# Attention scores: the low part of the keys padded with zero rows, so that both passes of a score use all 128 rows

## The chip, the cores and the metric

The kernel runs on one core of a Trainium2 chip. The metric is the device time of one execution in microseconds (us). Three runs of the kernel before took 2261.57, 2261.72 and 2266.63 us, so their median is 2261.72 us.

## The reference

The reference runs two blocks on 256 tokens x of 1024 features, the first of them together with 256 context tokens. All values are float32. The first block holds, in this order, a feed-forward layer, a differential attention, two more feed-forward layers, a neighbourhood attention and another feed-forward layer. The second block has two hybrid layers, which the change does not touch. The two attentions matter here:

```python
def _diff_attend(q, k, v, lam):                  # 8 heads, each with two halves j of 64 features
    s = jnp.einsum('bthjd,bkhjd->bhjtk', q, k)   # the scores
    p = jax.nn.softmax(s, axis=-1)
    p = p[:, :, 0] - lam * p[:, :, 1]
    return jnp.einsum('bhtk,bkhe->bthe', p, v)

# neighbourhood attention: 16 heads of 64 features, queries of x alone
s_lat = jnp.einsum('bqhd,brkhd->bhqrk', q, kb) + bias
s_ctx = jnp.einsum('bqhd,bchd->bhqc', q, kc)
p = jax.nn.softmax(concatenate([s_ctx, s_lat]))
```

In the differential attention the queries of x see 512 keys and those of the context see the 256 keys of the context. In the neighbourhood attention each query of x sees 512 keys.

## The kernel before

TensorE multiplies operands of the type float32r. A float32 value is held as the sum of two float32r parts, high and low, and a product takes three passes: high by high, high by low, low by high (`mm3`, L190; each matmul is issued in `mm`, L161, so most matmuls of the trace stand at L164).

A score has only 64 features to sum over, half of the 128 rows of the array. `stack` (L692) uses this to need two passes instead of three. For each half j of a pair of 64 features, the rows that the half owns are `own` (rows 0 to 63 for j = 0, rows 64 to 127 for j = 1). The tile `a` (named w in the trace) holds the high part of the query on the rows `own` and its low part on the other 64 rows. The tile `b` (also w) holds the high part of the key on both. The tile `kl` holds the low part of the key, on the rows `own` alone, for j = 0 and j = 1 in the two halves of the partitions of one [128, 512] tile. ScalarE makes the high parts (L699, L700, and the copy on the other rows, L703), VectorE makes the low parts by subtraction (L701, L702).

`score` (L706) then issues two matmuls into one PSUM bank. The first runs over all 128 rows and gives high by high plus low by high. The second takes the 64 rows `own` of `a` and of `kl` and gives high by low. In the trace they are `ac<-w` and `ac<-kl,w`.

In the differential attention (`diff_attention`, L730) each of 8 heads has four tiles of 128 queries and two halves, so 8 scores: four over 512 keys and four over 256. A head's work: `project` takes the finished projections of queries and keys out of PSUM (L743, L744), applies the rotary embedding on VectorE (L747 to L750) and calls `stack`; `values` transposes the previous head's probabilities (L200, L786) and multiplies them with the values (L179); `scores` issues the 8 scores with the maximum on VectorE (L765), the exponential on ScalarE (L766) and the normalisation on VectorE (L767 to L770). The generator `projections` issues the next head's projections (`ab<-u,w`, 48 matmuls a head), which the scheduler lays between the scores. Each engine runs its instructions in the order that is fixed when the program is built.

In the neighbourhood attention (`nb_attention`, L814) each of 8 head pairs has two tiles of queries and two heads, so 4 scores over 512 keys. The rest is alike: L825 and L826 take out the projections, L839 to L850 are the softmax, L864 takes out the transposes.

The memory of such a stage comes from a pool that is opened after the feed-forward layer before it; the first writes into it wait for the last readers of the tiles that lay there.

Of the kernel before, what the change touches and what calls it, by code (L numbers as in the profile page):

```python
# [23 lines left out]
F = mybir.dt.float32  # L24
R = mybir.dt.float32r
# [7 lines left out]
FA = 12  # L33
# [10 lines left out]
class Split:  # L44
    """A float32 operand held exactly as the sum of two float32r parts."""
# [8 lines left out]
class Sums:  # L54
    """sums of squares over the 1024 features of 256 tokens, from four parts [128, 2, 256]: the parts added
    up on the vector engine or, direct, on the tensor engine"""
# [27 lines left out]
class Net:  # L84
# [16 lines left out]
    @contextmanager  # L101
    def psum(self, **tags):
        """The PSUM banks of a phase: a number for each kind of use."""
        with ExitStack() as es:
            self.banks = self.pool(es, "ps" + "_".join(tags), 1, space=bass.MemoryType.PSUM)
            self.nbank = tags
            yield

    @contextmanager
    def space(self, name, n):  # L110
        """The 4 KiB tiles of a phase."""
        with ExitStack() as es:
            self.bp = self.pool(es, name, n)
            yield

    # ---- tiles
# [21 lines left out]
    # ---- weights: raw float32 from DRAM, then two float32r parts that sum to it  # L138
# [19 lines left out]
    # ---- products. A start clears the flags of its whole bank. Groups that share a bank are run one  # L158
    # after another (groups=0), or as one group (groups=n) whose first matmul alone has the start and
    # whose last alone the stop.  # L160
# [28 lines left out]
    # out += stat^T @ mov for every (out, mov), in three passes of float32r  # L189
# [12 lines left out]
    # ---- constants  # L202
# [27 lines left out]
    # ---- modulation vectors: ada_w^T silu(c) + ada_b, as columns  # L230
    def ada_first(self):
        """The first layer's first scale and the last quarter of its shift on the tensor engine, the rest of
        the shift on the vector engine. Returns x's norm factors."""
# [45 lines left out]
    def ada_chunks(self, l, mods):  # L279
        """Thunks, one for each 128 values of modulation, and one for each vector that adds the bias."""  # L280
# [31 lines left out]
    def spread(self, thunks, steps):  # L312
        """An iterator: each next() runs its share of the thunks."""
        thunks = list(thunks)
        done = 0
        for i in range(steps):
            want = -(-(i + 1) * len(thunks) // steps)
            while done < min(want, len(thunks)):
                thunks[done]()
                done += 1  # L320
            yield
        while True:
            yield

    # ---- norm factors as columns
    def pre_cols(self, l, which, j):
        """(1 + scale) * g and shift of sublayer `which` (0, 1, 2) for half j."""
        a = self.const([128, DT], f"pa{l}{which}{j}", tag=f"pa{which}{j}")
        self.nc.vector.scalar_tensor_tensor(a, self.mod[l][:, 3 * which + 1, :, j], 1.0, self.ng[l][:, 2 * which],
                                            op0=OP.add, op1=OP.mult)  # L330
        return a, self.mod[l][:, 3 * which, :, j]
# [7 lines left out]
    # ---- 1 / sqrt(sum of squares / n + eps) in every partition: a table's value and one Newton step  # L339
    def rstd(self, ss, n, p=None):  # L340
        """ss: tensors whose sum is to be summed over the partitions, if p, that sum in PSUM, isn't given"""
# [25 lines left out]
    def add_normed(self, y, r, cols, j):  # L367
        """h += cols * rmsnorm(y), y in two tiles [128, 4, 256]"""
# [12 lines left out]
    def table(self, x):  # L381
        """loads the table of the inverse root, once x is there"""
        self.nc.scalar.activation(self.col.tile([128, 1], F, name="tb", tag="tb", bufs=1), x, AF.Abs_reciprocal_sqrt)

    def new_u(self, n=2):
        """hi and lo of [1024, 256 n] features by tokens"""
# [16 lines left out]
    def normed(self, u, cols, shift, j, r=None, dve=False):  # L403
        """u = rmsnorm(h) * cols + shift in two parts"""
# [18 lines left out]
    def scaled(self, cols, shift=None):  # L423
        """h * cols of x in two parts, with shift's parts in the two columns that follow, if there is one, and
        the factors 1 / rms(h) of the tokens, along the free dimension in every partition"""
# [17 lines left out]
    def columns(self, r):  # L443
        """r as columns [128 tokens, 2]"""
# [7 lines left out]
    # ---- feed-forward  # L452
    def ffn(self, n, u, halves, mid, xdone, extra=(), r=None):
        """xdone(y) takes x's tiles of silu(a) * b @ w_out, then ctx's are worked out and returned.
        mid() is run when the work on x that needs nothing of ctx has been issued."""
# [51 lines left out]
        with self.space("ffn", 12):  # L507
# [19 lines left out]
            # the first FA features' share of y  # L527
# [11 lines left out]
            # the others', x before ctx  # L539
# [27 lines left out]
    # ---- shared parts of the mixers  # L567
# [10 lines left out]
    def projections(self, src, u, first):  # L578
        """starts the products of a mixer's queries (x's alone, if first is 1) and keys. The generator
        prefetches the weights of the next pair before it gives a pair's PSUM; the first pair's x comes  # L580
        apart, before ctx."""
# [20 lines left out]
    def v_tiles(self, src, u, mid, more):  # L602
        """token-major values [128 tokens, 1024] of the four token tiles, x's before mid()"""
# [31 lines left out]
    def out_proj(self, src, o, halves, xdone):  # L635
        """o(h, j) gives the pair [128, 256] of rows 128 h .. of the product's input for half j. The steps
        of the first quarter are given out, for use while o is still being made."""
# [52 lines left out]
    # ---- products of two 64-row operands, two to a tile: q = qh + ql stands on the rows of both halves,  # L690
    # so that one pass carries qh kh + ql kh and a second one qh kl
    def stack(self, q, k, tile_):  # L692
# [3 lines left out]
        kl = tile_((128, nk), "kl")  # L696
        for j in range(2):
# [4 lines left out]
            nc.vector.tensor_tensor(kl[own], k[own], b[own, j].bitcast(F), op=OP.subtract)  # L702
            nc.scalar.activation(b[other, j], k[own], AF.Copy)  # L703
        return a, b, kl

    def score(self, s, ops, j, q0, q1, k0, k1):  # L706
        a, b, kl = ops
        own = slice(64 * j, 64 * j + 64)
        self.mm(s, a[:, j, q0:q1], b[:, j, k0:k1], True, False)
        self.mm(s, a[own, j, q0:q1], kl[own, k0:k1], False, True)  # L710

    # ---- differential attention
# [17 lines left out]
    def diff_attention(self, u, mid, xdone):  # L730
        nc, I = self.nc, self.I
        with self.space("da", 1):
            rope = self.big((128, 2, 256), tag="rope")
            nc.sync.dma_start(rope, I["rope"].rearrange("a p t -> p a t"))
            rc, rs = [rope[:, i].unsqueeze(1).broadcast_to([128, 2, 256]) for i in range(2)]
            qks = self.projections(I["da_qk"], u, 2)
# [3 lines left out]
            def project():  # L740
# [10 lines left out]
                return self.stack(qk[:, 0], qk[:, 1],  # L751
                                  lambda shape, tag: self.bp.tile(list(shape), R, name=tag, tag=tag, bufs=1))
# [60 lines left out]
    # ---- neighbourhood attention (queries of x alone)  # L813
    def nb_attention(self, u, mid, xdone):  # L814
        nc, I = self.nc, self.I
        with self.space("na", 1):
            tile_ = lambda shape, tag, bufs, dt=F: self.bp.tile(list(shape), dt, name=tag, tag=tag, bufs=bufs)
            qks = self.projections(I["na_qk"], u, 1)
# [3 lines left out]
            def project():  # L822
# [4 lines left out]
                return self.stack(qk[:, 0:256], qk[:, 256:768], lambda shape, tag: tile_(shape, tag, 1, R))  # L827
# [64 lines left out]
    # ---- the second block's layer  # L892
    def softmax_small(self, rows, scale, bias, n, e):
        """softmax over n keys of scale * (the scores in PSUM + bias), into e"""
# [8 lines left out]
    def causal_pair(self, q, k, v, scale, bias, gate, x):  # L903
        """x [128, 256] = gate * the two heads' causal attention, a head in each 64 partitions:
        q(j), k(j) feature-major, v(j, tt) token-major [128, 64], bias(j, qt) over 128 (qt + 1) keys"""
# [24 lines left out]
    def second_consts(self):  # L930
# [12 lines left out]
        # sel[:, k] spreads row k of every block of 16 rows over the block  # L943
# [31 lines left out]
    def gates(self, ba, abt):  # L975
        """beta and the log decay of GDN, token-major [128 tokens, 2 tiles, 4 heads]"""
# [11 lines left out]
        # log1p(e) = ln(w) + (e - (w - 1)) / w with w = 1 + e  # L988
# [12 lines left out]
    def delta_rule(self, prn, cw, gates, abt, others):  # L1001
        """Returns U and the causal q k matrix: o^T = U^T A, by the two tiles of tokens."""
# [22 lines left out]
        # decays between tokens j <= t, then the two triangular matrices, transposed: [j, t]  # L1025
# [36 lines left out]
        # inverses of the diagonal blocks, dd = (1 + N)^-1 and ee its transpose: blocks of 16 column by column,  # L1062
        # row k of a block spread over the block's rows by the tensor engine, then larger ones from pairs
# [45 lines left out]
        # values token-major, then both blocks' solutions  # L1109
# [20 lines left out]
    def rope_pe(self, x, n):  # L1130
        """in place on partitions 64 .. 95 of x [128, n, 256]"""
# [9 lines left out]
    def hybrid(self, l, scaled, prm3):  # L1141
# [35 lines left out]
        # MLA  # L1177
# [46 lines left out]
        # MoBA: the one block is the queries' own, so it is causal attention with the T5 bias  # L1224
# [13 lines left out]
        # GDN output  # L1238
# [24 lines left out]
        # h += the heads' product, the last heads after all others  # L1263
# [16 lines left out]
    # ---- the whole  # L1280
# [40 lines left out]
    def first_block(self, es, on, ada):  # L1321
# [10 lines left out]
        with self.psum(ab=3, ac=4):  # L1332
            # silu(c) along the free dimension, in every partition
# [13 lines left out]
            # u of the next sublayer from the last one's y (or none), for one half  # L1347
# [67 lines left out]
# ---- layout on the host  # L1415
# [43 lines left out]
def layout(v):  # L1459
    """The kernel's input arrays from the reference's: moved values and constants of the shapes alone."""  # L1460
# [29 lines left out]
    # the bias of every (query, key) of x: a value of the table inside the window, else the reference's constant  # L1490
# [9 lines left out]
    # second block  # L1500
# [47 lines left out]
```

## Time and profile before

| | |
|---|---|
| median of 3 runs (lowest, highest) | 2261.72 us (2261.57, 2266.63) |
| span of the profiled execution | 2263.0 us |
| instructions | 33412 |
| TensorE matmuls (PE), busy | 2206.7 us, 98% |
| TensorE weight loads (PEld), busy | 1884.7 us, 83% |
| VectorE (DVE), busy | 1590.9 us, 70% |
| ScalarE (ACT), busy | 1121.4 us, 50% |
| GpSimd (POOL), busy | 4.4 us |
| differential attention, first to last score | 476.8 to 643.6 us of the span |
| neighbourhood attention, first to last score | 1498.8 to 1622.9 us of the span |

The page gives no time for the profiled execution beside its span of 2263.0 us; that lies 1.3 us above the median of the runs and inside their range. Each matmul has its own weight load, and loads overlap matmuls. Matmuls are pipelined, so the lengths of neighbouring ones overlap in the timeline; the distance from one matmul's start to the next one's tells more than the length of one.

### The profile page before, as it was taken

Reading aid. Unit: us, or ns where it says so; the run is one execution under the profiler, and the core shown is the slowest. Engines: PE = TensorE matmul, PEld = TensorE weight load, DVE = VectorE, ACT = ScalarE, POOL = GpSimd, SP = SyncE. Lnnn points to the kernel's source line nnn. Section 1 sums busy time; section 2 is a strip of 40 time slices with the busy share of each in tenths; the row PEclk is TensorE's granted clock in tenths of the full one; section 3 lists DMA queues with packets and bytes.
Section 4 is the critical chain, followed back from the end, with each engine's and each line's share of the span. In section 5 each row is a group of like instructions: output and inputs, shape, how many; then the busy total and the mean of one; then the engine's idle time right before and its main releaser. Section 6 shows DMA issues by size and latency. Waiting matters only on the chain.

```text
span 2263.0 us, 33412 instructions
## 1 busy us (share of the span) xinstructions
PE 2206.7 (98%) x13010; PEld 1884.7 (83%) x13010; DVE 1590.9 (70%) x2899; ACT 1121.4 (50%) x1841; POOL 4.4 (0%) x29
## 2 busy tenths in 40 slices
PE   7999999999999999999999999999999989999998
PEld 4888889876679988889988889977789989888986
DVE  7876665868869876767854454956666568977985
ACT  4332224667768322235632233667654448547744
POOL 0000000000000000000000000000000000000000
PEclk9999999999989999999999999999999999999999
DMA  8555553421124755544554553432235553324321
GB/s 304 196 185 188 180 183 131 145 93 47 38 93 134 235 197 190 195 166 150 177 187 151 175 167 131 149 130 85 94 134 184 177 170 121 113 75 137 121 98 56
DMA packets 96164, 332.75 MB, mean 147 GB/s; under 512 B 12772, under 2 KB 15462, under 8 KB 96008
## 3 DMA queue, kind: packets, MB, share of 16 engines
q1 hardware_dynamic: 96008, 330.64, 43.0%
q8 instruction: 102, 1.67, 0.3%
q14 instruction: 54, 0.44, 0.1%
HBM read 329.55 MB, written 1.05 MB: 146 GB/s over the span
## 4 chain that ended last, share of the span: by engine, by line
PE 85%; DVE 7%; ACT 5%; DMA 1%; issue 1%; SPq 0%; DVEq 0%; ACTq 0%
PE ab L164 39%; PE ac L164 17%; PE ac L168 7%; PE pj L164 5%; PE ab L179 5%; PE gd L164 3%; PE n L164 3%; PE ab L168 2%; DVE w L156 1%; PE at L164 1%; ACT w L155 1%; PE gd L168 1%; DVE y L375 1%; PE pj L168 1%; DVE h L379 1%
## 5 line engine op out<-in xcount | busy, mean ns | idle before, releaser
L155 ACT ACTIVATE w<-raw 128x1024 fp32r<-128x1024 f32 x466 | 489.4, 1053 | 792.7 <-PE ab L164 271.9
L164 PE MATMUL ab<-u,w 128*128 128x512 f32 (+2 forms) x4320 | 876.2, 362 | 4.1 <-ACT u L438 4.1
L164 PEld LDWEIGHTS ab<-u,w 128*128 128x128 f32 x4320 | 727.2, 189 | 133.2 <-issue 5.1
L156 DVE TENSOR_TENSOR w<-raw,w 128x1024 fp32r<-128x1024 f32 x466 | 567.1, 1219 | 321.8 <-ACT w L155 314.9
L164 PE MATMUL ac<-b,w 128*128 128x512 f32 (+1 forms) x1152 | 235.9, 366 | 0.0
L164 PEld LDWEIGHTS ac<-b,w 128*128 128x128 f32 x1152 | 195.6, 188 | 39.6
L168 PE MATMUL ac<-b,w 128*128 128x256 f32 x1680 | 200.6, 280 | 0.0
L168 PEld LDWEIGHTS ac<-b,w 128*128 128x128 f32 x1680 | 198.4, 188 | 0.8
L164 PE MATMUL pj<-u,w 128*128 128x256 f32 (+1 forms) x1200 | 159.4, 289 | 5.6 <-ACT u L438 4.4
L293 DVE SCALAR_TENSOR_TENSOR ra<-ra,cb 128x1024 f32<-128x1024 f32 x130 | 158.2, 1221 | 5.5 <-ACT cb L1342 2.2
L164 PEld LDWEIGHTS pj<-u,w 128*128 128x128 f32 (+1 forms) x1200 | 148.7, 191 | 10.7 <-ACT u L438 5.0
L179 PE MATMUL ab<-u,w 128*128 128x256 f32 x1152 | 147.6, 290 | 7.6 <-ACT u L155 6.2
L179 PEld LDWEIGHTS ab<-u,w 128*128 128x128 f32 x1152 | 144.2, 197 | 9.2 <-ACT u L155 6.5
L293 DVE SCALAR_TENSOR_TENSOR c<-ra,cb 128x1024 f32<-128x1024 f32 x98 | 118.7, 1218 | 11.9 <-ACT cb L1342 6.4
L484 DVE TENSOR_TENSOR s<-s,ab 128x512 f32<-128x512 f32 (+1 forms) x78 | 47.0, 603 | 90.7 <-PE ab L164 90.2
L164 PE MATMUL ac<-w,u 128*128 128x512 f32 x384 | 90.4, 393 | 0.0
L164 PE MATMUL n<-r,ones 128*128 128x256 f32 (+1 forms) x216 | 77.4, 470 | 7.5 <-DVE r L62 3.1
L164 PEld LDWEIGHTS ac<-w,u 128*128 128x128 f32 x384 | 71.7, 188 | 15.4 <-DVE u L156 0.4
L155 ACT ACTIVATE b<-s 128x512 fp32r<-128x512 f32 (+1 forms) x100 | 53.5, 535 | 26.9 <-DVE s L484 19.8
L156 DVE TENSOR_TENSOR b<-s,b 128x512 fp32r<-128x512 f32 (+1 forms) x100 | 56.2, 562 | 3.1 <-ACT b L155 2.9
L164 PEld LDWEIGHTS n<-r,ones 128*128 128x128 f32 x216 | 37.7, 203 | 21.4 <-DVE r L62 9.4
L64 ACT ACTIVATE r<-h 128x512 f32<-128x512 f32 x56 | 35.1, 628 | 31.7 <-DVE h L379 10.7
(289 smaller groups left out, 2311.2 us busy)
## 6 DMA issues: line engine op xcount, KB each, us to landing
raw<-in_fin SPq DMA_DIRECT2D x194, 512.0 KB, 3.3
raw<-in_fout SPq DMA_DIRECT2D x112, 512.0 KB, 3.3
ra<-in_ada SPq DMA_DIRECT2D x72, 512.0 KB, 4.3
ra<-in_ada0r SPq DMA_DIRECT2D x58, 512.0 KB, 3.3
raw<-in_w SPq DMA_DIRECT2D x54, 512.0 KB, 3.3
raw<-in_da_qk SPq DMA_DIRECT2D x16, 512.0 KB, 3.2
raw<-in_na_qk SPq DMA_DIRECT2D x16, 512.0 KB, 3.3
raw<-in_w2o SPq DMA_DIRECT2D x16, 512.0 KB, 3.2
```

The source lines that it names most:

```text
L64: net.nc.scalar.activation(s, x, AF.Square)
L155: self.nc.scalar.activation(hi, x, AF.Copy)
L156: self.anchor = self.nc.vector.tensor_tensor(lo, x, hi.bitcast(F), op=OP.subtract).ins.name
L164: return mm(out, lhsT, rhs, start=start, stop=stop)
L168: ins = mm(out, lhsT, rhs, start=start and "first" not in bank, stop=stop and bank["done"] == n)
L179: ins = mm(out, lhsT, rhs, start=start, stop=stop)
L293: ins = nc.vector.scalar_tensor_tensor(junk, w, 1.0, self.cb[:, j], op0=OP.mult, op1=OP.mult, accum_out=self.mod[l][:, m, t, j:j + 1])
L375: ins = nc.vector.scalar_tensor_tensor(yy[:, t], yy[:, t], cols[:, k:k + 1], r, op0=OP.mult, op1=OP.mult)
L379: last = nc.vector.tensor_tensor(hh, hh, yy, op=OP.add).ins.name
L484: nc.vector.tensor_tensor(s, s, pb, op=OP.mult)
```

## The change

The tile `kl` becomes [128, 2, 512], with a part of its own for each half j. It is allocated once for a whole stage by `low_keys`, which sets the 64 rows that the half does not own to zero, on GpSimd. `stack` writes the rows `own` of part j as before. `score` now gives the second pass all 128 rows: on the rows `own` the product is high by low as before, and on the other rows the low part of the query meets zeros. The diff also drops comments and docstrings, which leaves the lines empty; that part is left out here.

```diff
-    def stack(self, q, k, tile_):
+    def stack(self, q, k, kl):
         nc = self.nc
         nq, nk = q.shape[-1], k.shape[-1]
         a, b = [self.wp.tile([128, 2, n], R, name="w", tag="w") for n in (nq, nk)]
-        kl = tile_((128, nk), "kl")
         for j in range(2):
             own, other = slice(64 * j, 64 * j + 64), slice(64 - 64 * j, 128 - 64 * j)
             nc.scalar.activation(a[own, j], q[own], AF.Copy)
             nc.scalar.activation(b[own, j], k[own], AF.Copy)
             nc.vector.tensor_tensor(a[other, j], q[own], a[own, j].bitcast(F), op=OP.subtract)
-            nc.vector.tensor_tensor(kl[own], k[own], b[own, j].bitcast(F), op=OP.subtract)
+            nc.vector.tensor_tensor(kl[own, j], k[own], b[own, j].bitcast(F), op=OP.subtract)
             nc.scalar.activation(b[other, j], k[own], AF.Copy)
         return a, b, kl

+    def low_keys(self, n):
+        kl = self.bp.tile([128, 2, n], R, name="kl", tag="kl", bufs=1)
+        for j in range(2):
+            self.nc.gpsimd.memset(kl[64 - 64 * j:128 - 64 * j, j].bitcast(F), 0.0)
+        return kl
+
     def score(self, s, ops, j, q0, q1, k0, k1):
         a, b, kl = ops
-        own = slice(64 * j, 64 * j + 64)
         self.mm(s, a[:, j, q0:q1], b[:, j, k0:k1], True, False)
-        self.mm(s, a[own, j, q0:q1], kl[own, k0:k1], False, True)
+        self.mm(s, a[:, j, q0:q1], kl[:, j, k0:k1], False, True)
...
+            kl = self.low_keys(512)
             qks = self.projections(I["da_qk"], u, 2)
...
+            kl = self.low_keys(512)
             qks = self.projections(I["na_qk"], u, 1)
```

On PE, DVE, ACT and SP the instructions stand in the same order as before, and 96 matmuls have 128 rows in place of 64. GpSimd's queue is the only one with new instructions. Before, from the branch that starts its program to its end:

```order
L1543 UNCONDITIONAL_BRANCH
L945 COPY sel<-ident 128x1920
L1008 MEMSET xp 128x3 x24
L1543 UNCONDITIONAL_BRANCH
L1543 ISA
```

The same place in the changed kernel, where each of the two stages has two of the four new writes:

```order
L1550 UNCONDITIONAL_BRANCH
L710 MEMSET kl 64x512 x4
L952 COPY sel<-ident 128x1920
L1015 MEMSET xp 128x3 x24
L1550 UNCONDITIONAL_BRANCH
L1550 ISA
```

The four writes stand ahead of everything that GpSimd had to do after its start. The first two second-pass matmuls of each stage now wait for them as well.

## Rows read from the trace of the kernel before

**Rows 1.** The page, chain that ended last, by engine.
```profile
PE 85%; DVE 7%; ACT 5%; DMA 1%; issue 1%; SPq 0%; DVEq 0%; ACTq 0%
```
**Rows 2.** Busy time by head: length, PE, PEld, DVE, ACT, POOL, clock, DMA, GB/s.
```profile
476.70:498.82 22.12, 21.70 (x87) 14.62 (x88) 18.48 (x40) 17.67 (x36) 0.00 (x0) 1.00 0.15 48
...
544.36:567.15 22.79, 22.03 (x91) 15.27 (x91) 19.11 (x40) 17.19 (x35) 0.00 (x0) 1.00 0.13 47
...
612.78:636.18 23.40, 20.69 (x78) 13.64 (x79) 18.02 (x40) 17.78 (x37) 0.00 (x0) 0.91 0.00 1
```
**Rows 3.** Timeline of PE, differential attention: start, length, instruction.
```profile
522.79 0.50 PE L164 MATMUL ac<-kl,w 64*128 64x512 f32 x1
...
523.65 0.50 PE L164 MATMUL ac<-kl,w 64*128 64x512 f32 x1
...
524.71 3.93 PE L164 MATMUL ab<-u,w 128*128 128x512 f32 x16
528.47 0.28 PE L164 MATMUL ac<-w 128*128 128x256 f32 x1
528.68 0.38 PE L164 MATMUL ac<-kl,w 64*128 64x256 f32 x1
528.99 0.73 PE L164 MATMUL ab<-u,w 128*128 128x512 f32 x2
529.56 0.28 PE L164 MATMUL ac<-w 128*128 128x256 f32 x1
```
**Rows 4.** Timeline of PE just before the stage's first score.
```profile
465.67 5.67 PE L168 MATMUL ab<-u,w 128*128 128x256 f32 x46
```
**Rows 5.** Timeline of PEld, the weight loads of the same score.
```profile
528.25 0.19 PEld L164 LDWEIGHTS ac<-w 128*128 128x128 f32 x1
528.68 0.18 PEld L164 LDWEIGHTS ac<-kl,w 64*128 64x128 f32 x1 [0.24 <-issue]
```
**Rows 6.** The tile kl, its matmuls: count, shortest, median, longest ns, shapes.
```profile
L164 PE MATMUL ac<-kl,w x96: 379/492/792, 477.2 to 1622.4; 64*128 64x512 f32 x64, 64*128 64x256 f32 x32
```
**Rows 7.** Waits, 521.58 to 612.78 us: us in total, times, longest.
```profile
DVE w L701 <- ACT w L699: 6.2, 8, 1.1
...
DVE sm L767 <- ACT c L766: 4.3, 4, 1.1
DVE mx L765 <- PE ac L164: 3.2, 8, 0.5
```
**Rows 8.** Timeline of DVE, 537 to 541.6 us.
```profile
538.33 0.69 DVE L750 TENSOR_TENSOR qk<-qk,s 128x512 f32<-128x512 f32 x1
540.13 0.69 DVE L701 TENSOR_TENSOR w<-qk,w 64x512 fp32r<-64x512 f32 x1 [1.11 <-ACT w L699]
```
**Rows 9.** Timeline of ACT, the same stretch.
```profile
538.99 0.60 ACT L786 ACTIVATE pT<-ac 128x512 f32<-128x512 f32 x1 [2.96 <-PE ac L200]
```
**Rows 10.** Chain of waits in the neighbourhood attention: start, length, piece.
```profile
1546.35 0.92 PE ac L164 x2
...
1548.42 0.65 PE ac L164 x2
...
1550.94 1.70 PE ac L164 x4
...
1562.70 0.92 PE ac L164 x2
```
**Rows 11.** Busy time in one head pair there, columns as in rows 2.
```profile
1546.35:1562.70 16.35, 16.20 (x88) 11.81 (x88) 10.59 (x32) 12.42 (x32) 0.00 (x0) 1.00 0.28 98
```
**Rows 12.** Timeline of PE at the last head of the differential attention.
```profile
634.02 0.79 PE L164 MATMUL ac<-kl,w 64*128 64x512 f32 x2
```
**Rows 13.** Busy time around that, columns as in rows 2.
```profile
620.00:640.00 20.00, 17.29 (x69) 11.11 (x68) 14.51 (x33) 14.36 (x26) 0.00 (x0) 0.83 0.08 27
```
**Rows 14.** Groups of instructions on POOL: count, busy, mean ns, idle before.
```profile
L1008 POOL MEMSET xp<- 128x3 f32 x24 | 2.4, 101 | 490.0 <-DVE r L1013 231.7 <-PE ac L168 223.2 <-DVE w L989 8.0
L945 POOL COPY sel<-ident 128x1920 f32<-128x1920 f32 x1 | 1.8, 1791 | 1623.1 <-DVE na L842 1623.1
```

More of the change, by code (lines that the diff above doesn't have):

```diff
@@ L750, in project @@
                 nc.vector.tensor_tensor(qx, qx, sh, op=OP.add)
-                return self.stack(qk[:, 0], qk[:, 1],
-                                  lambda shape, tag: self.bp.tile(list(shape), R, name=tag, tag=tag, bufs=1))
+                return self.stack(qk[:, 0], qk[:, 1], kl)
             def scores(qk):
@@ L826, in project @@
                 nc.scalar.activation(qk[:, 256:768], pk, AF.Copy)
-                return self.stack(qk[:, 0:256], qk[:, 256:768], lambda shape, tag: tile_(shape, tag, 1, R))
+                return self.stack(qk[:, 0:256], qk[:, 256:768], kl)
             def scores(hp, qk):
```

## The prediction

> **What bounds the kernel now.** I read the chain that ended last first: 85% of it is PE [rows 1], so a change of PE's work counts in full unless another engine takes over. Next I cut the differential attention into heads and read each one's busy times: from 498.82 us on, five heads repeat within 0.1 us, each 22.8 us long, with PE busy for 22.0, DVE for 19.1 and ACT for 17.2 us [rows 2]. PE sets the pace there, but DVE has only 3.7 us to spare. In the neighbourhood attention a head pair takes 16.35 us, with PE at 16.2, ACT at 12.4 and DVE at 10.6 [rows 11]: much more room. Then I read PE's own timeline for the distance between starts, since busy times of pipelined matmuls overlap.
>
> **What a 64-row pass costs today.** The undisturbed slot comes first. Behind a second pass, 16 projections of 512 columns take 3.76 us (524.71 to 528.47) and two take 0.57 (528.99 to 529.56), so 14 more cost 3.19 us: 0.228 us from start to start, and the first slot is longer by 0.11. A run of 46 with 256 columns, its last one 0.28 long, gives (5.67 - 0.28) / 45 = 0.120 us [rows 3, 4]. Now a score over 256 keys: from its first pass at 528.47 over the second pass and two projections to the next score at 529.56 there are 1.09 us, where four undisturbed slots would take 2 x 0.120 + 2 x 0.228 = 0.70. The excess is 0.39 us. It lies on both sides of the 64-row pass: 0.21 to reach it instead of 0.12, 0.31 to leave it instead of 0.12, and the two projections after it take 0.57 instead of 0.46 [rows 3]. The weight loads tell why. The load of the 128-row pass starts at 528.25, ahead of its matmul at 528.47; that of the 64-row pass starts at 528.68, together with its own matmul and 0.21 us after the matmul before it, with 0.24 us of idle time ahead that no semaphore explains ("issue") [rows 5]. So the load is not made ahead when the shape changes from 128 to 64 rows, and likewise on the way back. Where scores over 512 keys follow each other, two second passes stand 0.86 us apart (522.79 and 523.65) against 2 x 0.228 = 0.46: an excess of 0.40 us.
>
> **The change part by part.** There are 96 second passes, 64 of 512 and 32 of 256 columns [rows 6]. The differential attention has 8 heads with four of each, the neighbourhood attention 8 head pairs with four of 512. With 128 rows in both passes I expect the plain slots. On PE that removes 32 x 0.40 + 32 x 0.39 = 25.3 us in the first stage and 32 x 0.40 = 12.8 us in the second, 38.1 us in all. The number of matmuls and of columns stays as it was.
>
> In the neighbourhood attention all four scores of a head pair lie on the chain (0.92 + 0.65 + 1.70 us for what would be 4 x 0.46), and the next pair's start at 1562.70 follows them [rows 10]. PE would need 16.35 - 1.60 = 14.75 us, still above ACT's 12.4, so I count the full 1.6 us for seven pairs, and half of it for the last, where no projections are left to issue: 7 x 1.6 + 0.8 = 12.0 us.
>
> In the differential attention DVE takes over. PE alone would need 22.8 - 4 x 0.40 - 4 x 0.39 = 19.6 us a head. DVE is busy for 19.1 and waits 1.55 for ScalarE's copies before the first subtraction (6.2 us over four heads), 1.08 for the last exponential and 0.80 for scores [rows 7], and 0.26 in small pieces. The waits for scores go. The wait for the exponential goes too, as the exponential queues on ACT behind the copy of the finished projection, and PE would finish that earlier. Of the 1.55, 1.11 is the first subtraction's: the rotary embedding ends at 538.33 + 0.69 = 539.02, and the copy that it feeds finds ACT busy until 539.59 with a transpose that had waited 2.96 us for PE [rows 8, 9]. With that gone about 0.44 comes back; the copy itself and the second one's wait stay, 1.11 together. DVE's cycle is then 19.11 + 1.11 + 0.26 = 20.5 us, above PE's 19.6. So each of the five heads gains 22.8 - 20.5 = 2.3 us and not 3.2: 11.5 us. The first head has DVE at 18.5 of 22.1; with the same waits left (1.4 to 1.9 us) it gains 1.7. The last two have PE less loaded and longer waits for scores [rows 2]; I give them 2.0 and 1.0. Together 16.2 us.
>
> The four writes of zeros are no operation of before. Two rows of GpSimd bound one: 0.10 us for 128x3 elements and 1.79 us for 128x1920 [rows 14]; by the columns written, 512 lie nearer the first, so I take 0.5 us, and 2 x 1.79 = 3.6 us a stage as the far end. They stand first in GpSimd's queue and wait only for the feed-forward layer before; the first reader comes at 477.2 us [rows 6], behind a run of projections that alone takes 5.67 us [rows 4]. I count nothing; without that cover it would be at most 7.2 us for both stages. They can't pay below nothing, as they only add writes. The subtractions write as many elements as before.
>
> The sum is 12.0 + 16.2 = 28.2 us. From the span of 2263.0 us that leaves 2234.8; the median of the runs is 1.3 us below the span, so I expect 2233.5 us.
>
> **A rule weighed against the rows.** In undisturbed streams all loads and matmuls use 128 rows, and a slot is 0.228 us; where loads are late, in the run of 512-key scores, it is half of 0.86, 0.43 us [rows 3]. So loads of 128 rows do overlap matmuls of 128 rows. The Trainium skill, "TensorE: Matmul & The Clock Gate", Part 3: Packing small matmuls, says instead that a weight load overlaps a running matmul only when the two use different row groups. By that rule full rows would keep every load exposed and the change would bring nothing, 2262 us; the trace disagrees with it, at 0.228 us a slot. The same part says that two matmuls on different row groups can run at the same time, which full rows give up. In the trace one pair of second passes stands so (two in 0.79 us at 634.02 [rows 12]), so what is given up is one slot, 0.23 us.
>
> **The rivals.**
> - All of PE's time comes back: DVE's remaining waits give way too, since they are waits for ACT and no work. 2261.7 - 38.1 = 2223.6 us. For it speaks that DVE's 19.1 us of work are under PE's 19.6; against it that the copies feed the subtractions directly.
> - DVE holds the first stage more firmly: only the waits for scores come back, 0.8 x 8 = 6.4 us, with 12.0 of the second stage. 2243.3 us. For it speaks the fixed order, in which one wait can slide into the next.
> - The change doesn't do what it says: the load is late for another reason than the number of rows, for one that the second pass loads the same tile `a` again. 2261.7 us. Against it: the load back to a projection, with another tile, is late too (0.31 us in place of 0.12 [rows 3]).
> - Slower: with less work a head, PE's clock falls. In the slice from 620 to 640 us PE was busy for 17.3 of 20 us and the granted clock was 0.83, so some 0.34 x 20 = 6.8 us ran at 1.2 GHz, the lower level [rows 13]. At that level PE's work takes twice as long, so the gain of 28 us is used up once 56 us of PE's time run at it; if all heads of the first stage had 10 us of it, the kernel would lose 8 x 5 = 40 us and end at 2273. Against it: PE would still work 19.6 of 20.5 us, 96%, and stretches with PE at 22.0 of 22.8 us, 97%, had a clock of 1.00 [rows 2].
>
> **How the numbers follow.** I give my forecast 0.56, all of PE's time 0.20, DVE's firmer hold 0.15, no effect 0.06, and the falling clock 0.03. The range from 2222 to 2246 us takes in the first three with 1 to 3 us around their times, and leaves out the last two. A measurement of this kernel tells about 0.3%, 6.8 us, from no change. Faster by more than that are the first three, 0.91; within it, 0.06; slower, 0.03.
>
> **What would show it.** In the changed trace the rows of the second passes read 128*128, their loads start ahead of their matmuls, and two second passes in a run of 512-key scores stand 0.46 us apart. A head of the differential attention takes about 20.5 us with DVE busy for 19.1, and DVE's waits for scores are nearly gone; a head pair of the neighbourhood attention takes about 14.75 us. GpSimd's writes end long before the first score. I am wrong if second passes still stand 0.8 us apart, if heads take under 20 or over 21.5 us, or if the clock of the heads in the middle falls below 1.00.

## The result and the profile after

The changed kernel takes 2234.07 us (median of four runs, 2233.54 to 2239.74), the kernel before 2263.83 us (2261.57 to 2266.63; a fourth run of it, 2265.94 us, has joined the three). The ratio is 0.987, with a 95% interval from 0.9857 to 0.9883: the kernel is faster by 1.3%. The profiled executions have spans of 2232.3 and 2263.0 us, 30.7 us apart.

The page of the changed kernel gives the chain that ended last, by engine:

```profile
PE 79%; ACT 9%; DVE 9%; issue 1%; DMA 1%; SPq 0%; DVEq 0%; ACTq 0%
```

PE holds 79% of the chain in place of 85% [rows 1]. PE's own timeline in the differential attention answers to [rows 3]: start, length, instruction.

```profile
518.80 0.39 PE L164 MATMUL ac<-kl,w 128*128 128x512 f32 x1
...
519.25 0.40 PE L164 MATMUL ac<-kl,w 128*128 128x512 f32 x1
...
524.24 0.28 PE L164 MATMUL ac<-w 128*128 128x256 f32 x1
524.35 0.29 PE L164 MATMUL ac<-kl,w 128*128 128x256 f32 x1
...
524.95 0.28 PE L164 MATMUL ac<-w 128*128 128x256 f32 x1
```

Two second passes of 512 keys stand 0.45 us apart (518.80 and 519.25), where it was 0.86. A score over 256 keys with two projections takes 0.71 us (524.24 to 524.95), where it was 1.09. The weight load of that score's second pass, in PEld's timeline, answers to [rows 5]:

```profile
524.24 0.19 PEld L164 LDWEIGHTS ac<-kl,w 128*128 128x128 f32 x1
```

The second pass's load now starts at 524.24, with the first pass's matmul and 0.11 us ahead of its own at 524.35. Before, it started together with its own matmul.

Busy times by stretch have the columns of [rows 2]: a head of the differential attention, its seventh head, its last head up to the end of the stage, and that whole stage; below them a head pair of the neighbourhood attention and everything after that stage.

```profile
538.06:558.43 20.37, 19.42 (x91) 14.99 (x91) 18.90 (x41) 16.99 (x35) 0.00 (x0) 1.00 0.15 52
...
599.16:619.02 19.86, 16.71 (x78) 12.50 (x78) 17.41 (x40) 16.34 (x34) 0.00 (x0) 1.00 0.00 1
...
619.02:641.80 22.78, 19.65 (x117) 16.27 (x116) 18.09 (x36) 18.34 (x32) 0.00 (x0) 0.93 0.40 139
...
466.20:641.80 175.60, 164.04 (x802) 128.42 (x801) 152.66 (x321) 140.94 (x277) 0.00 (x0) 0.99 0.17 61
...
1523.74:1539.11 15.37, 15.10 (x88) 11.81 (x89) 10.61 (x32) 12.33 (x32) 0.00 (x0) 1.00 0.31 104
...
1611.32:2223.53 612.21, 591.68 (x4452) 545.30 (x4450) 455.22 (x1006) 344.45 (x556) 2.38 (x24) 0.99 0.38 127
```

The same stretches of the kernel before, cut at the same PE instructions. Its head, its seventh head (23.27 us from matmul to matmul) and its pair stand in [rows 2, 11]:

```profile
635.98:660.76 24.78, 22.67 (x116) 17.79 (x115) 17.69 (x35) 17.80 (x30) 0.00 (x0) 0.81 0.37 128
...
465.21:660.76 195.55, 186.81 (x802) 132.56 (x800) 154.56 (x321) 143.49 (x277) 0.00 (x0) 0.97 0.16 54
...
1638.36:2254.23 615.87, 596.04 (x4452) 548.56 (x4450) 454.99 (x1006) 344.45 (x556) 2.36 (x24) 0.99 0.38 126
```

From such stretches the 30.7 us come apart as follows (us, each rounded by itself):

| stretch | predicted | measured |
|---|---|---|
| differential attention, first head and what stands ahead of it in the stage | 1.7 | 2.3 |
| its next five heads (114.06 to 101.80) | 11.5 | 12.3 |
| its seventh head | 2.0 | 3.4 |
| its last head, to the end of the stage | 1.0 | 2.0 |
| neighbourhood attention (149.33 to 141.20) | 12.0 | 8.1 |
| everything after it | 0 | 3.7 |
| start of the program | 0 | -1.0 |
| sum | 28.2 | 30.7 |

The time came out within 0.6 us of the 2233.5 us predicted; the gain is 29.8 us between the medians, where 28.2 were predicted. That it comes so close is luck in part: one term is 3.9 us too large, others that are too small make up for it, and one of these, the 3.7 us behind the attentions, is not the change's (shown below).

The matmuls of tile `kl`, and GpSimd's writes, answer to [rows 6, 14] (count; shortest, median, longest ns; first and last start):

```profile
L164 PE MATMUL ac<-kl,w x96: 278/392/632, 478.1 to 1595.2; 128*128 128x512 f32 x64, 128*128 128x256 f32 x32
L710 POOL MEMSET kl<- x4: 519/522/525, 403.3 to 1412.4; 64x512 f32 x4
```

The first write starts at 403.3 us and takes 0.52, the first reader starts at 478.1. Nothing waits for the writes.

### The profile page after: what moved, and what is told of

Its sections match the earlier page's. It is cut to its first block, busy times and chain, and to the rows that moved or that the text cites. A ratio compares the mean times of both kernels' runs of the same rounds, so it can differ in the third digit from the quotient of the medians.

```text
span 2232.3 us, 33427 instructions
## 1 busy us (share of the span) xinstructions
PE 2169.9 (97%) x13010; PEld 1876.6 (84%) x13010; DVE 1589.2 (71%) x2899; ACT 1118.0 (50%) x1841; POOL 6.5 (0%) x33
## 4 chain that ended last, share of the span: by engine, by line
PE 79%; ACT 9%; DVE 9%; issue 1%; DMA 1%; SPq 0%; DVEq 0%; ACTq 0%
PE ab L164 36%; PE ac L164 16%; PE ac L168 7%; PE pj L164 5%; PE ab L179 5%; PE gd L164 3%; PE n L164 2%; PE ab L168 2%; ACT w L155 2%; DVE w L156 1%; PE at L164 1%; DVE y L375 1%; ACT c L772 1%; PE gd L168 1%; PE pj L168 1%
## 5 line engine op out<-in xcount | busy, mean ns | idle before, releaser
L293 DVE SCALAR_TENSOR_TENSOR c<-ra,cb 128x1024 f32<-128x1024 f32 x98 | 118.8, 1220 | 12.9 <-ACT cb L1349 6.4
```

Of the source, the lines that this page charges most:

```text
L293: ins = nc.vector.scalar_tensor_tensor(junk, w, 1.0, self.cb[:, j], op0=OP.mult, op1=OP.mult, accum_out=self.mod[l][:, m, t, j:j + 1])
```

## Experiments

**The mechanism: is it the change of shape, or the 64 rows?** This kernel is the one before, with the first pass on 64 rows as well. It leaves out the product of the query's low part with the key's high part.

```diff
-        self.mm(s, a[:, j, q0:q1], b[:, j, k0:k1], True, False)
+        self.mm(s, a[own, j, q0:q1], b[own, j, k0:k1], True, False)
         self.mm(s, a[own, j, q0:q1], kl[own, k0:k1], False, True)
```

> The kernel before with 64 rows in the first pass as well; it leaves out the product of the low part of the query with the high part of the key. Theory (the change of shape makes the load late): the second pass follows the first within 0.23 us at 512 columns and 0.12 at 256, while the late load moves to the first pass of a score that follows a projection (0.33 us and 0.43 us around it), and in a run of 512-key scores second passes stand 0.46 us apart or less. Rival (a load of 64 rows is late by itself): the second pass still follows the first by 0.33 to 0.43 us at 512 columns and 0.21 at 256, and second passes in a run stand 0.86 us apart. Second rival (loading the same tile again makes it late): as the first rival.

It took 2249.87 us (one run, against a median of 2264.5 for the kernel before). PE's timeline where scores over 512 keys follow each other, and at a score over 256 keys with two projections:

```profile
1543.09 0.50 PE L164 MATMUL ac<-w 64*128 64x512 f32 x1
1543.43 0.39 PE L164 MATMUL ac<-kl,w 64*128 64x512 f32 x1
...
1543.89 0.39 PE L164 MATMUL ac<-kl,w 64*128 64x512 f32 x1
...
528.03 0.38 PE L164 MATMUL ac<-w 64*128 64x256 f32 x1
...
529.12 0.38 PE L164 MATMUL ac<-w 64*128 64x256 f32 x1
```

Second passes of 64 rows stand 0.46 us apart (1543.43 and 1543.89), as those of 128 rows do. So 64 rows cost nothing by themselves, and neither does loading the same tile `a` twice. The score over 256 keys takes 1.09 us (528.03 to 529.12), just as in the kernel before: between projections it still enters the 64-row shape once and leaves it once. What costs is that the shape changes from one matmul to the next. The expectation missed two numbers: the step from a first pass that itself follows another shape to its second pass takes 0.34 us at 512 columns (1543.09 to 1543.43), not 0.23, and 0.22 at 256, not 0.12, which by itself would suit the rival's 0.21. Both are longer by some 0.1 us, as the first slot of a run of projections was by 0.11 in the kernel before; I read it as the first slot behind a late load. The Trainium skill, "TensorEngine Tiling (Array Packing)", Tiling Modes, Key Properties, says that a change of the tiling mode drains the engine, without a figure. The rows agree that a change costs time; whether it is a drain or only a load that isn't made ahead, they don't tell.

The same trace shows what a 64-row pass can do that a padded one cannot. The order of PE's instructions in this kernel differs from that of the kernel before, and 20 times two passes on different halves of the rows start together, here at 611.75 us:

```profile
611.75 0.49 PE L164 MATMUL ac<-kl,w 64*128 64x512 f32 x1
611.75 0.38 PE L164 MATMUL ac<-w 64*128 64x256 f32 x1
```

In the kernel before that happened once. Whether 64-row passes put side by side on purpose would beat the zero rows, no run tried.

**The two stages apart.** In the first kernel only the differential attention has the padded `kl`, in the second only the neighbourhood attention. The first one's core:

```diff
     def nb_attention(self, u, mid, xdone):
...
-            kl = self.low_keys(512)
...
+                kl = tile_((128, 512), "kl", 1, R)
                 return self.stack(qk[:, 0:256], qk[:, 256:768], kl)
```

> Only the differential attention has the zero-padded low keys; the neighbourhood attention keeps its 64-row second pass. Theory (a weight load is late at each change between 128 and 64 rows; VectorE then sets the head): a head of this stage takes 20.4 us as with the whole change, a head pair of the neighbourhood attention stays at 16.36 us, and 16 to 20 us of the 30 us come back, so some 2244 to 2248 us; of that, the part above 16 us is time at the lower clock that does not occur. Rival (the stages share a cause, such as the larger tile or the GpSimd writes): neither stage alone shows its whole part.

> Only the neighbourhood attention has the zero-padded low keys. Theory: a head pair takes 15.4 us as with the whole change, a head of the differential attention stays at 22.8 us, and about 8 us come back: 2255 to 2257 us; together with the other half it gives the whole change within 3 us. Rival (the 12 us that I had predicted for this stage are there, but hidden by something that the first stage's change moves): 2251 to 2252 us.

The first took 2246.51 us, ratio 0.9923 with an interval from 0.9907 to 0.994, a gain of 18.0 us; the second 2258.33 us, 0.9971 (0.9959 to 0.9983), a gain of 6.2 us (somewhat less than expected), both against 2264.5. A head of the first kernel:

```profile
537.40:557.76 20.36, 19.45 (x91) 14.97 (x91) 18.90 (x41) 16.97 (x35) 0.00 (x0) 1.00 0.16 52
```

and a head pair of the second:

```profile
1545.10:1560.47 15.37, 15.10 (x90) 11.81 (x88) 10.60 (x31) 12.33 (x32) 0.00 (x0) 1.00 0.33 104
```

Each stage gains on its own what it gains in the whole change, to 0.01 us a head or pair, and the stage that is not edited keeps its 22.79 or 16.36 us. The two gains add up to 24.2 us, though, and the whole change had 29.8 between medians, where a difference within 3 us was expected. Each gain is uncertain by about 3 us, so noise alone could make up much of these 5.6 us; the profiles tell more.

**Those 5.6 us: both kernels again.** Neither kernel is edited; each runs once more with a profile.

> The kernel before once more, for the time at the lower clock (1.2 GHz) behind 700 us, in work that the change does not touch. Theory (what that work gains, 3.6 us between the two profiles, comes from the clock and follows the chance of an execution): the stretches with the lower clock differ from the first profile's, and the time from the end of the neighbourhood attention to the last matmul, 615.9 us there, follows them at about a third of a us for each us. Rival (the change itself does it): the same stretches and the same 615.9 us.

> The changed kernel once more, for the same. Theory: heads of 20.36 us and head pairs of 15.37 us again, but other stretches with the lower clock, so that the time from the end of the neighbourhood attention to the last matmul differs from 612.2 us. Rival (the change does it): 612.2 us again.

They took 2265.86 and 2240.0 us. The part behind the neighbourhood attention took 615.90 and 614.09 us in them. A kernel from further below, which is the changed one without one multiplication in the differential attention, gives for that part:

```profile
1612.78:2228.00 615.22, 594.88 (x4452) 547.94 (x4450) 455.22 (x1006) 344.41 (x556) 2.37 (x24) 0.99 0.40 126
```

Heads and pairs repeat (20.37 and 15.37 us in the changed kernel). The rest does not. PE's instructions in that part, and their order, are the same in all the executions below; the time at the lower level is added up over the pieces with a granted clock of 0.50.

| kernel | the part's length (us) | of it at 1.2 GHz (us) |
|---|---|---|
| before, its two executions | 615.9, 615.9 | 17.1, 20.5 |
| only the neighbourhood attention changed | 615.6 | 20.5 |
| changed, its two executions | 612.2, 614.1 | 6.8, 17.1 |
| changed, without one multiplication | 615.2 | 17.1 |
| only the differential attention changed | 613.3 | 10.2 |
| changed, without table loads | 612.7 | 6.8 |
| before, with 64 rows in both passes | 612.7 | 6.8 |

So the part's 3.7 us go with the lower level of the clock and not with the padding: the kernel whose passes all have 64 rows gets down to 612.7 us, and a kernel with padded keys is back at 615.2. The repeat of the kernel before missed its expectation in one thing: the time at the lower level differs (20.5 for 17.1 us), but the part took 615.9 us again, so there is no fixed price for each us. The neighbourhood attention varies likewise: it took 141.20 us with 3.4 us at the lower level in the first execution of the changed kernel, and 142.65 with 6.8 in the second.

**What sets the head's 20.4 us, VectorE?** My prediction said that VectorE takes over. This kernel leaves out one multiplication of the rotary embedding, so VectorE has 0.7 us less to do a head. The kernels with one stage changed kept the order of instructions of the changed kernel. This one and the four that follow do not: on PE, VectorE and ScalarE the order is laid anew when the program is built. They differ by more than their edit, then, and what a head waits for has to be read from each one's own trace.

```diff
                 nc.vector.stream_shuffle(sh, qx, SWAP)
-                nc.vector.tensor_tensor(sh, sh, rs, op=OP.mult)
                 nc.vector.tensor_tensor(qx, qx, rc, op=OP.mult)
```

> The whole change, without one multiplication of the rotary embedding (0.69 us on VectorE a head; the rotary embedding's sine part is left unscaled). Theory (VectorE with its waits for ScalarE's copies sets the head at 20.36 us, TensorE would allow 19.6): a head falls to 19.7 us. Rival (TensorE still sets it): a head stays at 20.3 to 20.4 us. The neighbourhood attention stays at 15.37 us a head pair.

One run took 2238.63 us. A head, and below it the wait of the subtractions for ScalarE's copies over four heads (us in total, times, longest), first in this kernel:

```profile
537.75:558.10 20.35, 19.63 (x91) 14.96 (x90) 18.18 (x40) 17.00 (x35) 0.00 (x0) 1.00 0.17 52
...
DVE w L700 <- ACT w L698: 7.6, 8, 1.5
```

then in the changed kernel:

```profile
ACT pT L792 <- PE ac L200: 12.9, 8, 3.0
DVE w L700 <- ACT w L698: 4.7, 8, 0.8
```

VectorE is busy for 18.18 us in place of 18.90, and the head still takes 20.35. What was taken from its work came back as waiting: 2.9 us more over four heads, 0.72 a head. The chain through one head of this kernel holds pieces of PE and ScalarE and none of VectorE. VectorE's work does not set the head.

**ScalarE's queue, first way.** One of the three copies that ScalarE makes for each half goes to GpSimd.

```diff
-            nc.scalar.activation(b[other, j], k[own], AF.Copy)
+            nc.gpsimd.tensor_copy(b[other, j], k[own])
```

> The whole change, and the copy of the key's high part to the other 64 rows (two a head) moved from ScalarE to GpSimd. Theory (in the neighbourhood attention the chain now runs through ScalarE's queue, where the transposes' copies stand behind four copies of 0.63 us, and in the differential attention VectorE waits 0.43 us a head for the second half's copy): the head pair falls from 15.4 towards 14.8 us and the head from 20.4 to about 19.9, some 6 us in all, about 2228 us. Rival (GpSimd takes much longer than ScalarE's 0.63 us for the copy, or slows VectorE down while it writes): no gain, or up to 15 us lost, 2234 to 2250 us.

This took 2223.72 us (2222.11 to 2225.41), ratio 0.982 with an interval from 0.9806 to 0.9835: it beats both kernels. The interval lies wholly below that of the change. The expectation had 2228 us. One head, one pair, and from the chain through the head (start, length, piece) the first and the last of VectorE's pieces and what follows:

```profile
534.89:554.73 19.84, 19.34 (x91) 15.08 (x90) 18.86 (x41) 16.07 (x33) 1.70 (x2) 1.00 0.16 54
...
1513.41:1528.43 15.02, 15.02 (x89) 11.77 (x88) 10.66 (x32) 11.40 (x30) 1.22 (x2) 1.00 0.35 105
...
531.92 0.69 DVE w L700
...
544.80 0.67 DVE c L776
545.51 0.56 PE ac L200 x3
```

VectorE has the same work as in the changed kernel, 18.86 us, and the head is shorter by 0.52 us. In the pair PE is busy throughout, 15.02 of 15.02. The head's chain has moved: from 531.92 to 545.51 us it runs on VectorE nearly without a break, where that of the changed kernel (below) runs on ScalarE for the most part. Not all of the 10 us between the medians are in heads and pairs: of the 7.8 us by which the first stage is shorter in the profiles, 3.8 are in its last two heads, which had no time at 1.2 GHz here and 3.4 us in the changed kernel.

**ScalarE's queue, second way.** In the norm of a head's output the inverse root is replaced by the exponential, so that ScalarE need not load a table twice a head.

```diff
-    def rstd(self, ss, n, p=None):
+    def rstd(self, ss, n, p=None, fn=AF.Abs_reciprocal_sqrt):
...
-        nc.scalar.activation(r, p, AF.Abs_reciprocal_sqrt, bias=self.eps, scale=1.0 / n)
+        nc.scalar.activation(r, p, fn, bias=self.eps, scale=1.0 / n)
...
-                r = self.rstd(self.square(po, 512), 128)
+                r = self.rstd(self.square(po, 512), 128, fn=AF.Exp)
```

> The whole change, with the exponential in place of the inverse root in the heads' norm of the differential attention, so that ScalarE doesn't change its function table twice a head (2 x 1.28 us); the norm's factor is then wrong. The fifth run left a head at 20.36 us with 0.69 us less on VectorE. Theory (ScalarE's queue sets the head: it is busy for 17.0 of 20.36 us, and its other 3.2 us are one wait for transposes that come late on TensorE): the head falls, to VectorE's cycle of 19.1 us of work and 1.2 us of waits, about 20.2, if that one is nearly as long, or to TensorE's 19.6 us if it is not. Rival (something else, say TensorE's own work, is the floor at 20.36 us): the head stays within 0.05 us.

One run took 2233.43 us, and a head 19.86:

```profile
536.00:555.86 19.86, 19.26 (x91) 14.89 (x91) 18.52 (x41) 14.63 (x33) 0.00 (x0) 1.00 0.17 54
```

ScalarE is busy for 14.63 us in place of 16.99, and the head loses 0.51 us, about as with the moved copies; of the two lengths expected, 20.2 and 19.6, it is neither. The whole run shows little of it (2234.07 us is the changed kernel's median): the neighbourhood attention, which the edit does not touch, took 142.8 us in place of 141.2. Two different cuts in ScalarE's queue shorten the head, a cut in VectorE's work alone does not. ScalarE is never full, though: it works 17.0 of 20.4 us and waits 12.9 / 4 = 3.2 a head for PE's transposes. It is in the way by where its work stands. Pieces of the chain through one head of the changed kernel show it (start, length, piece), and below them PE's two waits in that head, from its timeline:

```profile
539.66 1.28 ACT L353
...
541.66 1.28 ACT L772
542.96 2.12 ACT c L772 x6
```

```profile
548.56 0.87 PE L200 MATMUL ac<-ident,c 128*128 128x128 f32 x6 [0.59 <-DVE c L776]
...
549.79 1.13 PE L179 MATMUL ab<-pT,v 128*128 128x256 f32 x4 [0.36 <-ACT pT L792]
```

Table loads (1.28 us each, L353 and L772), the exponentials (c), the copies of the transposes (pT) and the copies for the scores (w) follow each other on ScalarE, and PE and VectorE come between. PE stands idle for 0.95 us of the head: 0.59 until VectorE has normalised what PE is to transpose, behind ScalarE's exponentials, and 0.36 until ScalarE has copied the transposes. That is all that parts 19.42 from 20.37 us. With the copies moved or without the table loads PE no longer waits for VectorE; 0.36 or 0.60 us for the copy of the transposes are left.

**Both cuts at once.** The kernel without the table loads, without the rotary multiplication as well.

> The edits of the fifth and the ninth run together: no table loads in the heads' norm and one multiplication of the rotary embedding less (both results are wrong for it). Theory (two cycles of nearly the same length, one through ScalarE's queue and one through VectorE's): only with both shortened the head falls to TensorE's 19.6 us or a little under. Rival (TensorE's own work is the floor at 20.36 us): the head stays within 0.05 us.

```profile
534.99:554.87 19.88, 19.37 (x91) 14.87 (x90) 17.92 (x40) 14.62 (x33) 0.00 (x0) 1.00 0.17 54
...
546.55 1.99 PE L179 MATMUL ab<-pT,v 128*128 128x256 f32 x8 [0.37 <-ACT pT L791]
```

The expectation missed: one run took 2228.15 us, but the head stays at 19.88, with VectorE at 17.92 and ScalarE at 14.62. PE's timeline shows one wait in it, the last line: 0.37 us for ScalarE's copy of the transposes, which PE itself has just made. So PE takes about 19.5 us for its instructions in this order, close to the 19.6 that it was to need by itself, and this wait comes on top. The run as a whole is shorter than the one before by 5.3 us, which is about what its last two heads lose (43.2 to 37.5 us).

**More for GpSimd.** To the moved copies this kernel adds one multiplication of the rotary embedding on GpSimd.

```diff
-                nc.vector.tensor_tensor(qx, qx, rc, op=OP.mult)
+                nc.gpsimd.tensor_tensor(qx, qx, rc, op=OP.mult)
```

> The copy on GpSimd as in the fourth run, and one more multiplication of the rotary embedding moved there from VectorE. Theory (with the copy moved, VectorE still sets the head of 19.84 us, TensorE is at 19.6): a head falls by 0.2 to 0.3 us to TensorE's 19.6, about 2 us in all, 2221 to 2222 us. Rival (GpSimd takes longer than the 0.69 us that it saves, and the subtraction chain behind it waits): a head of 20 us or more, 2225 us or more.

It took 2231.42 us (2230.46 to 2232.06), ratio 0.9859 (0.9843 to 0.9876), slower than with the copies alone, as the rival had it. A head, and the multiplication:

```profile
537.24:557.66 20.42, 19.58 (x91) 14.97 (x90) 19.05 (x40) 15.99 (x33) 2.50 (x3) 1.00 0.15 52
...
L756 POOL TENSOR_TENSOR qk<-qk,rope 128x512 f32<-128x512 f32 x8 | 11.1, 1391 | 177.5 <-DVE s L754 162.5 <-DVE sm L773 14.9
```

It takes 1.39 us where VectorE needs 0.69, and the head goes back to 20.42 us. That the multiplication's 0.7 us more show in the head almost in full (0.58), since it stands between the projection and the copies, is argued; the order of the other engines differs as well.

## Why the prediction was right or wrong

**The excess of a 64-row pass: right.** Predicted were 0.40 and 0.39 us, measured are 0.86 - 0.45 = 0.41 and 1.09 - 0.71 = 0.38 in the differential attention, and loads of 128 rows are made ahead. The run with both passes at 64 rows shows that it is the change of shape. The rule of the Trainium skill on loads ("TensorE: Matmul & The Clock Gate", Part 3) would have kept the time as it was; at 0.23 us from pass to pass the rows after disagree with it as those before did.

**The neighbourhood attention: a term mis-sized, 12.0 for 8.1 us** (6.7 between the second executions of both kernels). The step that failed is "all four scores of a head pair", each at 0.40: I carried the excess over from the other stage. PE's timeline of one pair, before:

```profile
1546.35 0.49 PE L164 MATMUL ac<-w 128*128 128x512 f32 x1 [0.16 <-ACT w L703]
...
1547.20 1.22 PE L164 MATMUL ab<-u,w 128*128 128x256 f32 x8
1548.26 0.39 PE L164 MATMUL ac<-w 128*128 128x512 f32 x1
...
1549.00 1.94 PE L164 MATMUL ab<-pT,v 128*64 128x256 f32 x14
```

and after:

```profile
1523.74 0.50 PE L164 MATMUL ac<-w 128*128 128x512 f32 x1 [0.16 <-ACT w L702]
...
1524.31 1.11 PE L164 MATMUL ab<-u,w 128*128 128x256 f32 x8
1525.53 0.50 PE L164 MATMUL ac<-w 128*128 128x512 f32 x1
1525.86 0.40 PE L164 MATMUL ac<-kl,w 128*128 128x512 f32 x1
1526.19 1.94 PE L164 MATMUL ab<-pT,v 128*64 128x256 f32 x14
1528.06 0.50 PE L164 MATMUL ac<-w 128*128 128x512 f32 x1
...
1529.09 7.53 PE L164 MATMUL ab<-u,w 128*128 128x256 f32 x40
```

The chain at the second score there (start, length, piece):

```profile
1525.00 0.49 ACT pT L871
...
1525.53 0.73 PE ac L164 x2
```

The first score takes 0.57 us where it took 0.85. The second takes 0.66 where it took 0.74: behind it come the values, whose loads are 64 columns wide (128*64), so the shape still changes there, and the slot into them stays at 0.33. The third and fourth, behind those values, take 1.03 where they took 1.70 [rows 10]. Together that is a gain of 1.03 us, not 1.60. Then 0.16 are lost: the second score starts 1.22 us after the eight projections ahead of it and not 1.06, because by the chain it waits there for ScalarE's copy of the transposes, a wait that I had left out. The run of 40 projections is shorter by 0.11. That makes the 0.98 us a pair that are seen (16.35 to 15.37). [Rows 10] had the 0.65 of the second score, already less than the 0.92 of the first, and I took one price for both. With the copies on GpSimd a pair takes 15.02 us with PE never idle, so even then, in that kernel's order, PE needs more than the 14.75 that I had.

**The differential attention: the number right, the reason wrong.** "DVE takes over" failed. I had 20.5 us a head, and 20.4 came out, but VectorE's work and waits always add up to the head's length; that they do is no proof that VectorE sets it. Without 0.7 us of its work the head stays as it is, and with 0.9 us less (two copies moved) or 2.4 us less (no table loads) on ScalarE it is 0.5 shorter, though each of these kernels has an order of its own. What I said of the waits held: those for scores and for the exponential [rows 7] are no longer listed, and the subtractions wait 4.7 / 4 = 1.18 us a head, where I had 1.11. What holds the head of the changed kernel is a chain mostly through ScalarE's queue, with PE at 19.4 of 20.4. VectorE is not far behind: where two copies have left that queue, the chain of the head of 19.84 us runs on VectorE.

**The last two heads: 3.4 and 2.0 in place of 2.0 and 1.0 us.** These two were set without a sum, and too low. Part of the difference may be the clock's. Before, the granted clock was 0.91 on average in the seventh head and 0.81 in the last, which means 2 x 0.09 x 23.27 = 4.2 and 2 x 0.19 x 24.78 = 9.4 us at the lower level of 1.2 GHz; after, it was 1.00 and 0.93, so none and 2 x 0.07 x 22.78 = 3.2. How much of the gain that makes is not shown: the second execution of the changed kernel had twice as much of it in the last head, and its stage took 175.88 in place of 175.60 us. The slower rival asked for the clock to fall with less work on PE; it rose here, and in the heads in the middle it stayed at 1.00.

**What I costed at nothing.** For the writes that held: they take 0.52 us each (I took 0.5) and end, in the first stage, some 74 us before the first score. The part after the attentions, which I left at zero, moved by 3.7 us; the table above puts these down to the clock and not to the change.

**The rivals.** PE's time did not all come back: that needed heads of 19.6 us, and even the version with the copies on GpSimd has 19.84. A firmer hold would have kept the heads near 22. No effect is excluded by the slots.

## What to carry to other kernels

Price a change of a matmul's shape by the distance from start to start, at each place by its own neighbours: padding one operand with zeros pays in full only where the matmuls on both sides have the full shape, too (here 0.4 us, and 0.08 us ahead of loads of 64 columns). Where an engine's busy time and waits add up to the period, take some work off it before you believe that it sets the period: here it was for the most part another engine's queue, and moving two short copies from it to an idle engine gave a further 10 us between medians. Read what an engine waits for in its own timeline, and see whether a variant kept the order of instructions before you compare it.

## What the runs showed of the hardware beside that

The first slot after a late load is 0.11 us longer than the next (0.34 for 0.23 us at 512 columns). Two 64-row passes on different halves of the rows can start at the same time (both at 611.75 us in the kernel with 64 rows in both passes). GpSimd's copy of 64x512 elements takes 0.74 us against ScalarE's 0.63, and its multiplication of 128x512 is 1.39 us, twice VectorE's 0.69: here moving the copy paid, moving the multiplication did not. One and the same run of PE's instructions took from 612.2 to 615.9 us, with 6.8 to 20.5 us at the lower level of the clock.
